# Two gate tiles of the merge projection move from direct products into a thirteenth seven-product pair

## The chip, the cores and the metric

The kernel runs on one core of one Trainium2 chip. The metric is the device time of one execution in microseconds; the number for a kernel is the median of its runs. The profiled execution is a single one, and its page and trace are those of the hardware profiler.

## The reference

One transformer block over 1024 positions of width 1024, in fp32. The part that matters here:

```python
u = rms_norm(h, g_norm_mix[l])
proj = jnp.einsum('btd,de->bte', u, w_in[l]) + b_in[l]
mq, mk, mv, mo, mi, mf, nq, nkv, ngate, merge = split_columns(proj, IN_SIZES)
y_m = mlstm_mixer(mq, mk, mv, mo, mi, mf, b_fgate[l], conv_qk[l], g_mlstm_head[l])
y_n = nsa_mixer(nq, nkv, ngate, pe_cmp[l], w_cmp1[l], w_cmp2[l], rel_bias)
ys = jnp.stack([y_m, y_n], axis=2)
branch = jnp.einsum('btnw,nwd->btnd', ys, w_branch[l])
gates = jax.nn.sigmoid(merge.reshape(B, T, N_BRANCH, D_MODEL))
mixed = jnp.sum(gates * branch, axis=2)
h = h + mixed @ w_out[l]
```

Behind it come a normalised feed-forward layer with three more projections and a last normalisation. `merge`, 2048 columns of the input projection, is the subject: 16 tiles of 128 columns each, needed only when the two branches (mLSTM rows y_m, attention rows y_n) are gated.

## The kernel before

Every fp32 product is made of three passes in a reduced fp32 format: operands are split into a high part (a copy by ACT, ScalarE) and a low part (the rest, by DVE, VectorE), and `mm3` (lines 310 to 313) issues high x high, low x high and high x low. A *direct* tile of 128 columns is 2 halves of 512 positions x 8 slices of depth x 3 matmuls. A *pair* is two such tiles (256 columns) by a Strassen-like scheme: seven products of half the depth (order `QO`: 1, 2, 6, 7, 5, 4, 3), each of 4 slices x 3 matmuls, with sums of weight blocks made beforehand (`sums`, `prep`) and sums of results afterwards (`product`, `finish`), on DVE.

The work runs in stages.

1. **Stage A** (to about 300 us): normalisation, then the twelve pairs in `PAIRS` (line 784), whose two raw weight blocks go to the slots in `RAWS` (line 788) and whose split operands go round a ring of four slots, `WRING`. Beside the pairs run the gates, the compression of keys, and row broadcasts `d_rep` (line 1249, after product 5 of pairs 2 to 9). A planner (`Plan`, line 78) orders all steps by ranks, estimated costs and readiness, engine by engine, when the program is built; each engine then runs its queue in that order, and so does SP's queue, which issues nearly all DMAs. PE is TensorE, POOL is GpSimd.
2. **Heads of the mLSTM** (to about 370 us), same planner. Merge tile 0 is made in stage A; tiles 1 to 3 (`merge_B`, line 1379) are *fill* here: steps of 3 matmuls that the planner puts into PE's holes. Their raw weights go to slot r2, their split parts to the operand ring.
3. **Attention** (to about 680 us): 32 units in an order written out by a second planner (from line 1685): scores, exponentials, scaling, then per group of blocks transposes on PE (tile `T`, two buffers), the high part on ACT (`TH`), the low part on DVE (`TL`), and the products with the values in `obank`. A unit's result goes over `os` to `d_yn` (line 1677). Merge tiles are fill again: `c_dense` (line 1512) yields 16 steps for each of NMC = 10 tiles, `place_dense` (line 1832) puts a step where the planner's clock has PE idle for over 120 ns, and what is left over is issued behind the last unit (line 1902).
4. **Branch stage** (stage D, from line 1950): the remaining two merge tiles, 14 and 15, run first. Into their steps `plan_y` (line 1979) sets the loads and splits of the rows: `load_y(k)` reads the rows y0 to y3 (mLSTM, one part each) and y4 to y7 (attention, two parts each, added by `split_y`) into a ring of six slots; `split_y(k)` makes `YH` on ACT and `YL` on DVE in two halves. `load_gates` reads back the stored merge tiles. Then the products of the branches: `FIRST` (line 2015) is the order for output tiles 0 and 1, all b = 0 products (rows y0 to y3) ahead of the b = 1 products (y4 to y7); `gate` multiplies with the sigmoid on DVE. The tiles 2 to 7 follow one by one.
5. **Output projection, feed-forward, last normalisation** (from line 2080), by the planner again.

The weights of the direct tiles in stages 3 and 4 come through one stream (`Stream`, line 233): a raw load on SP, the high part on ACT, the low part on POOL or DVE.

Of the kernel before, what the change touches and what calls it, by code (L numbers as in the profile page):

```python
# [8 lines left out]
F32 = mybir.dt.float32  # L9
# [5 lines left out]
P = 128  # L15
# [11 lines left out]
C_MQ, C_MK, C_MV, C_MO, C_MI, C_MF = 0, 512, 1024, 1536, 2048, 2052  # L27
C_NQ, C_KV, C_NG, C_MG = 2056, 2568, 3336, 3360
# [6 lines left out]
EPS = 1.0e-6  # L35
MM = 216.0
NTH = 3
NMB, NMX, NMC = 4, 0, 10
FB_ = 400
FB2_ = 1  # L40
NZ_ = 4
# [144 lines left out]
def body(ctx, tc, a, out, stop=None, dbg=None):  # L186
# [113 lines left out]
    def wcols(w, c, n=P):  # L300
        return w.rearrange("(k p) c -> p k c", p=P)[:, :, c:c + n]
# [31 lines left out]
    def wu(ap, scale=None):  # L333
        return ws.add(ap, (KT, P), None, scale)

    j_mg = [wu(wcols(win, C_MG + P * j)) for j in range(16)]
    wbr = a["w_branch"].rearrange("n (k p) c -> p (n k) c", p=P)
    j_br = [wu(wbr[:, :, P * d:P * d + P]) for d in range(8)]

# [23 lines left out]
    with ExitStack() as sa:  # L363
# [417 lines left out]
            load("SP", 256, [(d_mg[t][:, ts_], lambda: o.ap)], [o], [K(True)])  # L781

        QO = (1, 2, 6, 7, 5, 4, 3)
        PAIRS = [("n", 0), ("c", 0), ("q", 0), ("n", 1), ("k", 0), ("s", 0), ("q", 1), ("v", 0), ("k", 1), ("v", 1), ("o", 0), ("o", 1)]
        NP = len(PAIRS)
        COL0 = {"n": C_NQ, "c": C_KC, "q": C_MQ, "k": C_MK, "v": C_MV, "o": C_MO}
        ROW0 = {"n": R_NQ, "q": 0, "k": 4, "v": 8, "o": R_MO}
        RAWS = ["r1 r2", "r0 g20", "g10 r1", "r2 r0", "g20 g10", "r1 r2", "r0 g20", "g10 r1", "r2 r0", "g20 g10", "r1 r2", "r0 g20"]
        WRING = ("w0", "w2", "w1", "w3")
        RB, SB_, OB, keep = {}, {}, {}, {}  # L790
        LO, HI = slice(0, P), slice(P, 2 * P)
# [71 lines left out]
        def store(kb, parts, b, d):  # L863
            load("SP", kb, parts, [b] if isinstance(b, Buf) else b, [d])

        def finish(m, blk, ps, other):
            kind, z = PAIRS[m]
            col, r = blk
            j = 2 * z + col
            bias = COLS[:, R_KV + (col, (2, 4)[col])["cs".index(kind)]:][:, 0:1] if kind in "cs" else COLS[:, ROW0[kind] + j:ROW0[kind] + j + 1]  # L870
            pv, ov = (lambda: ps.ap), (lambda: other.ap)

            def total(cost, view, x):
                o = (lambda: four(other.ap)) if kind in "qk" else ov
                stt(cost, view, (lambda: four(ps.ap)) if kind in "qk" else pv, bias, o, ALU.add, ALU.add, [ps, other, b_c], [x])
            if kind in "qk":
                if (m, col) not in wt:
                    wt[m, col] = slot(order4[turn.setdefault(m, 0)])
                    turn[m] += 1
                w = wt[m, col]  # L880
                total(800.0, lambda: par(flat(w.ap), r), w)
                if (m, col, 1 - r) in wt:
                    conv(m, col)
                wt[m, col, r] = True
                return
            x = out_piece(m)
            v = lambda: x.ap
            if kind == "o":
                ew(V, v, pv, ov, ALU.add, [ps, other], [x])
                stp("ACT", 630.0, lambda: nc.scalar.activation(x.ap, x.ap, AF.Sigmoid, bias=bias), [ps, b_c, tabs[-1]], [x])  # L890
                store(256, [(par(d_mx["o"][j], r), lambda: four(x.ap))], x, dst["o", j])
            else:
                total(760.0, v, x)
                if kind in "cv":
                    d_, db = (d_kc[col], dstc[col]) if kind == "c" else (d_mx["v"][j], dst["v", j])
                    store(256, [(par(d_, r), lambda: four(x.ap))], x, db)
                else:
                    y = out_piece(m, 1)
                    f = -0.125 if kind == "n" else 1.0
                    stp("ACT", 630.0, lambda: nc.scalar.activation(fr(y.ap), x.ap, AF.Copy, scale=f), [x], [y])  # L900
                    if kind == "n":
                        stt(900.0, lambda: fr(x.ap), v, f, lambda: y.ap, ALU.mult, ALU.subtract, [y], [x])
                        ds_, db = [d_q[j][:, zz, :] for zz in range(2)], dstq[j]
                    else:
                        ew(V, lambda: fr(x.ap), v, lambda: y.ap, ALU.subtract, [y], [x])
                        ds_, db = [d_kh[col], d_kl[col]], dsts[col]
                    for d_, t_ in zip(ds_, (y, x)):
                        store(256, [(par(d_, r), lambda t_=t_: four(t_.ap))], t_, db)
            turn[m] += 1
# [325 lines left out]
        for n, (m, q) in enumerate(seq):  # L1235
            kind = PAIRS[m][0]
            if n > 1:
                if q == 1 and n > 13:
                    if m == 2:
                        bias_rows()  # L1240
                        load_raw(2)
                    load_raw(m + 1)
                prep(m, q)
            if (m, q) == (NP - 2, 1):
                table("sigmoid_and_others")
                stp("ACT", 340.0, lambda: nc.scalar.activation(GT[:, :, 0:24], GT[:, :, 0:24], AF.Sigmoid), tabs[-1:], [b_GT])
                stp("DVE", 1360.0, lambda: nc.vector.reciprocal(GT[:, :, 0:24], GT[:, :, 0:24]), (), [b_GT])
            product(m, q)
            if q == 5 and 1 < m < NP - 2:
                load("SP", 983, [(d_rep[m - 2], d_row[m - 2, :].partition_broadcast(P))], [OB[m, q], b_drow], [K(True)], cost=700.0)  # L1250
            if (m, q) == (NP - 1, 4):
                restore()
            if (m, q) == (3, 3):
                compress_0()
                compress(0)
            if (m, q) == (5, 3):
                compress(1)
            if (m, q) == (8, 3):
                head_load(0, "MqkS")
                mask(0)  # L1260
                scale_q(0)
            if (m, q) == (NP - 2, 7):
                head_load(0, "v")
# [656 lines left out]
    def q1_tile(n, dt):  # L1920
        if n not in q1 or q1[n].dtype != dt:
            q1[n] = q1p.tile([P, 4, 512], dt, name=f"q1_{n}_{len(q1)}", tag=f"q1_{n}", bufs=1)
        return q1[n]
# [24 lines left out]
    with ExitStack() as se:  # L1948
# [1 line left out]
        psD = se.enter_context(tc.tile_pool(name="psD", bufs=1, space=PSUM, reuse_waits="tile"))  # L1950
        YH = dp.tile([P, 8, T], F32R, name="YH")
        YL = dp.tile([P, 8, T], F32R, name="YL")
        ring = [q1_tile(n, F32)[:, 2 * z:2 * z + 2, :].rearrange("p a c -> p (a c)") for n in (4, 0, 1) for z in range(2)]
        ys, sgs = {}, {}

        def load_y(*kk):
            for k in kk:
                ys[k] = []
                for src in [d_ym[k]] if k < 4 else [d_yn[0][k - 4], d_yn[1][k - 4]]:
                    ys[k].append(ring.pop(0))  # L1960
                    ring.append(ys[k][-1])
                    nc.sync.dma_start(ys[k][-1], src[:, :])

        def split_y(k):
            y, *more = ys.pop(k)
            for y2 in more:
                nc.vector.tensor_tensor(y, y, y2, ALU.add)
            for half in range(2):
                hs = slice(512 * half, 512 * half + 512)
                split_evict(YH[:, k, hs], YL[:, k, hs], y[:, hs])  # L1970

        def load_gates(d, half):
            hs = slice(512 * half, 512 * half + 512)
            sgs[d, half] = [gring.tile() for b in range(2)]
            for b in range(2):
                nc.sync.dma_start(sgs[d, half][b], d_mg[8 * b + d][:, hs])

        early = Pieces([q1_tile(3, F32)[:, z, :] for z in range(4)])
        plan_y = {(0, 0): [lambda: load_y(0, 1, 2, 3)], (0, 2): [lambda: load_y(4)], (0, 8): [lambda: split_y(0)],
                  (0, 10): [lambda: split_y(1), lambda: load_y(5)], (0, 13): [lambda: split_y(2)], (1, 1): [lambda: split_y(3), lambda: load_y(6)],  # L1980
                  (1, 7): [lambda: split_y(4), lambda: load_y(7)], (1, 12): [lambda: split_y(5)]}
        for n, j in enumerate(range(NMB + NMX + NMC, 16)):
            for z, _ in enumerate(merge_tile(j, gring, psD, 8)):
                for f in plan_y.get((n, z), ()):
                    f()
                if (n, z) == (1, 9):
                    gring, late = early, gring
                    for half in range(2):
                        load_gates(0, half)
                    gring = late  # L1990
# [27 lines left out]
        for d in range(2):  # L2018
            W[d] = ws.get(j_br[d])
        ws.dma(j_br[2])  # L2020
        split_y(6)
        for n, (d, half, b) in enumerate(FIRST):
            x = branch(d, half, b)
            if n == 0:
                split_y(7)
            if n == 6:
                ws.split(j_br[2])
                ws.dma(j_br[3])
            gate(d, half, b, *x)
            if n == 5:  # L2030
                gring.n = 0
                gring, late = early, gring
                load_gates(2, 0)
                gring = late
# [873 lines left out]
```

## Time and profile before

| | |
|---|---|
| median of 3 runs | 1520.71 us (1520.65 to 1521.54) |
| the profiled execution | 1521.38 us |
| its span, first to last instruction | 1519.6 us |
| PE busy | 1507.8 us (99%), 8112 matmuls |
| DVE busy | 1176.0 us (77%) |
| ACT busy | 852.1 us (56%) |
| POOL busy | 174.5 us (11%) |
| moved by DMA | 207.54 MB, 137 GB/s in the mean |

The page gives the busy time of each engine, the span in 40 slices, the DMA queues, the chain of work that ended last (followed back from the last instruction), and groups of instructions. Views of the trace answer closer questions: a table by windows (busy time of each engine between two times), a timeline by engine (start, duration, line, tiles, and in brackets the idle time before and what ended it), and the groups of one tile. Matmuls overlap in the pipe, so a row shows 0.39 us for a matmul while the next starts 0.23 us later. In a row, `d` is the PSUM tile of a direct merge tile in stages 3 and 4, `mg` its evicted result in attention, `br` a branch product, `q` any tile of the ring that the y rows and gates share.

### The profile page before, as it was taken

To read this page: it belongs to the slowest core of one execution; us is meant where nothing else is said; L and a number is where in the kernel's file an instruction comes from. 1 tells how busy PE (TensorE), PEld (TensorE's weight loads), DVE (VectorE), ACT (ScalarE), POOL (GpSimd) and SP (SyncE) were. 2 spreads that over 40 slices of the span, in tenths; PEclk is the share of its full clock that TensorE was granted. 3 is DMA by queue.
4 is the path that set the end of the run, shared out by engine and by line. 5 is a ranking of instruction groups with operands and counts; after the bars stand their busy time and mean duration, and the time that the engine had idled before them with its cause. 6 is when DMAs were issued, how large, how long until landed. Compare 5 with 4: busy or idle time off the path is not lost.

```text
span 1519.6 us, 23351 instructions
## 1 busy us (share of the span) xinstructions
PE 1507.8 (99%) x8112; PEld 1297.1 (85%) x8112; DVE 1176.0 (77%) x2464; ACT 852.1 (56%) x1873; POOL 174.5 (11%) x310
## 2 busy tenths in 40 slices
PE   9999999999999999999999999999999999999997
PEld 8978888888988889888888888888888888888886
DVE  7877889466988798965666598677777778898976
ACT  8535444475988788865444364444444444564443
POOL 7600003333111100011020000000000000110000
PEclk9999999999999999999999999999999999999999
DMA  8458567869232533118456222222222226866002
GB/s 252 156 138 246 190 190 248 227 224 260 76 89 70 156 73 90 41 53 297 139 181 201 84 70 84 76 84 83 84 86 88 84 87 200 282 155 206 1 1 111
DMA packets 164144, 207.54 MB, mean 137 GB/s; under 512 B 10555, under 2 KB 121016, under 8 KB 163771
## 3 DMA queue, kind: packets, MB, share of 16 engines
q1 hardware_dynamic: 152090, 188.22, 38.7%
q0 software_dynamic: 11648, 17.51, 5.9%
q8 instruction: 64, 1.05, 0.3%
q14 instruction: 54, 0.43, 0.1%
q10 hardware_dynamic: 288, 0.33, 0.1%
HBM read 151.34 MB, written 62.48 MB: 141 GB/s over the span
## 4 chain that ended last, share of the span: by engine, by line
PE 96%; DVE 2%; DMA 1%; ACT 1%; issue 1%; DVEq 0%; ACTq 0%; POOLq 0%
PE PS L2323 41%; PE PSA L311 7%; PE PSA L313 6%; PE PSA L312 6%; PE T L1636 4%; PE d L311 3%; PE d L313 3%; PE d L312 3%; PE obank L1667 2%; PE obank L1669 2%; PE PS L313 2%; PE PS L311 2%; PE br L313 2%; PE br L312 2%; PE PS L312 2%; PE br L311 2%
## 5 line engine op out<-in xcount | busy, mean ns | idle before, releaser
L2093 DVE TENSOR_TENSOR sl<-PS,sl 128x512 f32<-128x512 f32 (+1 forms) x186 | 101.2, 559 | 46.2 <-PE PS L2323 32.4
L2323 PE MATMUL PS<-sl,sl 128*128 128x512 f32 (+1 forms) x597 | 129.3, 371 | 0.0
L2323 PEld LDWEIGHTS PS<-sl,sl 128*128 128x128 f32 x597 | 105.8, 188 | 19.5 <-DVE acc L2093 0.2
L1656 DVE TENSOR_TENSOR TL<-T,TH 128x512 fp32r<-128x512 f32 (+1 forms) x151 | 90.6, 617 | 19.3 <-ACT TH L1647 17.6
L2096 ACT ACTIVATE sl<-PS 128x512 f32<-128x512 f32 x72 | 43.0, 598 | 98.5 <-PE PS L2323 96.3
L2096 ACT ACTIVATE sl<-sl 128x512 fp32r<-128x512 f32 (+1 forms) x91 | 56.7, 629 | 70.1 <-DVE sl L2093 48.4
L1647 ACT ACTIVATE TH<-T 128x512 fp32r<-128x512 f32 (+1 forms) x151 | 79.3, 540 | 18.8 <-PE T L1636 17.3
L1667 PE MATMUL obank<-TH,VHL 128*128 128x256 f32 x263 | 75.6, 310 | 0.0
L2093 DVE TENSOR_TENSOR sl<-sl,sl 128x512 fp32r<-128x512 f32 (+1 forms) x90 | 61.6, 686 | 17.4 <-DMA d_h<-sl 8.7
L2323 PE MATMUL PS<-UTH,wl 128*128 128x512 f32 (+1 forms) x272 | 74.8, 346 | 0.0
L311 PE MATMUL d<-UTH,whi 128*128 128x512 f32 x176 | 71.4, 406 | 0.1
L2323 PE MATMUL PS<-q,wh 128*128 128x512 f32 x300 | 70.8, 389 | 0.0
L313 PE MATMUL d<-UTH,wlo 128*128 128x512 f32 x176 | 69.1, 393 | 0.0
L312 PE MATMUL d<-UTL,whi 128*128 128x512 f32 x176 | 69.1, 392 | 0.0
L1669 PE MATMUL obank<-TL,VHL 128*128 128x256 f32 x264 | 68.3, 282 | 0.0
L311 PE MATMUL PSA<-UTH,wOwhi 128*128 128x512 f32 (+1 forms) x172 | 67.1, 390 | 0.0
L313 PE MATMUL PSA<-UTH,wOwlo 128*128 128x512 f32 (+1 forms) x180 | 66.9, 371 | 0.0
L2323 PEld LDWEIGHTS PS<-q,wh 128*128 128x128 f32 x300 | 56.3, 188 | 11.7
L2323 PE MATMUL PS<-UTH,wh 128*128 128x512 f32 (+1 forms) x248 | 66.1, 338 | 0.0
L312 PE MATMUL PSA<-UTL,wOwhi 128*128 128x512 f32 (+1 forms) x172 | 63.7, 370 | 0.0
L2323 PE MATMUL PS<-q,wl 128*128 128x512 f32 x252 | 59.7, 389 | 0.0
L2323 PE MATMUL PS<-q,sl 128*128 128x512 f32 x240 | 57.2, 389 | 0.0
(1389 smaller groups left out, 4561.1 us busy)
## 6 DMA issues: line engine op xcount, KB each, us to landing
d_gu<-sl SPq DMA_DIRECT2D x44, 256.0 KB, 2.3
rA<-in_w_in SPq DMA_DIRECT2D x18, 512.0 KB, 5.6
q<-d_mg SPq DMA_DIRECT2D x32, 256.0 KB, 3.4
d_rep<-d_row SPq DMA_DIRECT2D x8, 960.0 KB, 7.8
ra<-in_w_gate SPq DMA_DIRECT2D x14, 512.0 KB, 5.0
sl<-in_w_up SPq DMA_DIRECT2D x13, 512.0 KB
raw<-in_w_in SPq DMA_DIRECT2D x10, 512.0 KB, 4.9
d_mg<-mg SPq DMA_DIRECT2D x20, 256.0 KB, 2.1
```

The costliest lines, as they stand in the source:

```text
L311: nc.tensor.matmul(ps, ah, bh, start=first, stop=False)
L312: nc.tensor.matmul(ps, ah, bl, start=False, stop=False)
L313: nc.tensor.matmul(ps, al, bh, start=False, stop=last)
L1636: nc.tensor.transpose(pt[:, z, P * r:P * r + P], e, ident)
L1647: nc.scalar.activation(hl[0][:, 0:m], pt[:, 0:m], AF.Copy)
L1656: nc.vector.tensor_tensor(hl[1][:, 0:m], pt[:, 0:m], cast32(hl[0])[:, 0:m], ALU.subtract)
L1667: nc.tensor.matmul(po, vv, th[:, z, :], start=(st[1] == 0), stop=False)
L1669: nc.tensor.matmul(po, vv, tl[:, z, :], start=False, stop=(st[1] == st[2]))
L2093: return pl.step(alts, lambda e: ENG[e].tensor_tensor(out_(), x(), y(), alu), reads, writes, **kw)
L2096: return pl.step((("ACT", cost),), lambda e: nc.scalar.activation(out_(), x(), fn), reads, writes, **kw)
L2323: nc.tensor.matmul(ps, x, y, start=first and n == 0, stop=last and n == 2, skip_group_check=True)
```

## The change

Merge tiles 14 and 15 become pair `("g", 0)` of stage A, between `("k", 1)` and `("v", 1)`: thirteen pairs in place of twelve. Its results get the bias in the sum on DVE and are stored to `d_mg[14]` and `d_mg[15]`. The raw slots of the last pairs shift by one place, so that the last pair uses r1 and r2. Of the tiles 4 to 13, nine (4 to 12) are fill of attention, and one (13) runs at the head of the branch stage. The y rows get a ring of eight slots; y4 and y5 are loaded at once behind y0 to y3, y6 and y7 within the one tile; y0 to y4 are split within it, y5 ahead of the first branch product, y6 behind the first and y7 behind the third. The bank from which the planner of stage 5 starts counting (`n0`, line 2084) follows NMC: 6 in place of 4.

```diff
-NMB, NMX, NMC = 4, 0, 10
+NMB, NMX, NMC = 4, 0, 9
+MG2 = 14
...
-    j_mg = [wu(wcols(win, C_MG + P * j)) for j in range(16)]
+    j_mg = [wu(wcols(win, C_MG + P * j)) for j in range(MG2)]
...
-        PAIRS = [..., ("v", 0), ("k", 1), ("v", 1), ("o", 0), ("o", 1)]
+        PAIRS = [..., ("v", 0), ("k", 1), ("g", 0), ("v", 1), ("o", 0), ("o", 1)]
...
-        RAWS = [..., "g20 g10", "r1 r2", "r0 g20"]
+        RAWS = [..., "g20 g10", "r1 r2", "r0 g20", "r1 r2"]
...
+            bias = COLS[:, R_MG + MG2 + col:R_MG + MG2 + col + 1] if kind == "g" else ...
...
-                if kind in "cv":
+                if kind == "g":
+                    store(256, [(par(d_mg[MG2 + col], r), lambda: four(x.ap))], x, K(True))
+                elif kind in "cv":
...
-            if q == 5 and 1 < m < NP - 2:
+            if q == 5 and 1 < m < 10:
...
-        ring = [... for n in (4, 0, 1) for z in range(2)]
+        ring = [... for n in (4, 0, 1, 2) for z in range(2)]
...
-        plan_y = {(0, 0): [lambda: load_y(0, 1, 2, 3)], (0, 2): [lambda: load_y(4)], (0, 8): [lambda: split_y(0)],
-                  (0, 10): [lambda: split_y(1), lambda: load_y(5)], (0, 13): [lambda: split_y(2)], (1, 1): [lambda: split_y(3), lambda: load_y(6)],
-                  (1, 7): [lambda: split_y(4), lambda: load_y(7)], (1, 12): [lambda: split_y(5)]}
-        for n, j in enumerate(range(NMB + NMX + NMC, 16)):
+        plan_y = {(0, 0): [lambda: load_y(0, 1, 2, 3)], (0, 2): [lambda: load_y(4, 5)], (0, 6): [lambda: split_y(0)],
+                  (0, 8): [lambda: split_y(1), lambda: load_y(6)], (0, 10): [lambda: split_y(2)], (0, 12): [lambda: split_y(3), lambda: load_y(7)],
+                  (0, 14): [lambda: split_y(4)]}
+        for n, j in enumerate(range(NMB + NMX + NMC, MG2)):
...
-                if (n, z) == (1, 9):
+                if (n, z) == (0, 9):
                     gring, late = early, gring
                     for half in range(2):
                         load_gates(0, half)
...
-        split_y(6)
+        split_y(5)
         for n, (d, half, b) in enumerate(FIRST):
             x = branch(d, half, b)
-            if n == 0:
-                split_y(7)
+            if n in (0, 2):
+                split_y((6, 7)[n // 2])
```

More of the change, by code (lines that the diff above doesn't have):

```diff
@@ L783, in body @@
         QO = (1, 2, 6, 7, 5, 4, 3)
-        PAIRS = [("n", 0), ("c", 0), ("q", 0), ("n", 1), ("k", 0), ("s", 0), ("q", 1), ("v", 0), ("k", 1), ("v", 1), ("o", 0), ("o", 1)]
+        PAIRS = [("n", 0), ("c", 0), ("q", 0), ("n", 1), ("k", 0), ("s", 0), ("q", 1), ("v", 0), ("k", 1), ("g", 0), ("v", 1), ("o", 0), ("o", 1)]
         NP = len(PAIRS)
-        COL0 = {"n": C_NQ, "c": C_KC, "q": C_MQ, "k": C_MK, "v": C_MV, "o": C_MO}
+        COL0 = {"n": C_NQ, "c": C_KC, "q": C_MQ, "k": C_MK, "v": C_MV, "o": C_MO, "g": C_MG + P * MG2}
         ROW0 = {"n": R_NQ, "q": 0, "k": 4, "v": 8, "o": R_MO}
-        RAWS = ["r1 r2", "r0 g20", "g10 r1", "r2 r0", "g20 g10", "r1 r2", "r0 g20", "g10 r1", "r2 r0", "g20 g10", "r1 r2", "r0 g20"]
+        RAWS = ["r1 r2", "r0 g20", "g10 r1", "r2 r0", "g20 g10", "r1 r2", "r0 g20", "g10 r1", "r2 r0", "g20 g10", "r1 r2", "r0 g20", "r1 r2"]
         WRING = ("w0", "w2", "w1", "w3")
@@ L869, in finish @@
             j = 2 * z + col
-            bias = COLS[:, R_KV + (col, (2, 4)[col])["cs".index(kind)]:][:, 0:1] if kind in "cs" else COLS[:, ROW0[kind] + j:ROW0[kind] + j + 1]
+            bias = COLS[:, R_MG + MG2 + col:R_MG + MG2 + col + 1] if kind == "g" else COLS[:, R_KV + (col, (2, 4)[col])["cs".index(kind)]:][:, 0:1] if kind in "cs" else COLS[:, ROW0[kind] + j:ROW0[kind] + j + 1]
             pv, ov = (lambda: ps.ap), (lambda: other.ap)
@@ L1952, in body @@
         YL = dp.tile([P, 8, T], F32R, name="YL")
-        ring = [q1_tile(n, F32)[:, 2 * z:2 * z + 2, :].rearrange("p a c -> p (a c)") for n in (4, 0, 1) for z in range(2)]
+        ring = [q1_tile(n, F32)[:, 2 * z:2 * z + 2, :].rearrange("p a c -> p (a c)") for n in (4, 0, 1, 2) for z in range(2)]
         ys, sgs = {}, {}
```

## The prediction

> **What bounds the kernel now.** I read the page's head and chain first.
>
> ```profile
> span 1519.6 us, 23351 instructions
> ...
> PE 96%; DVE 2%; DMA 1%; ACT 1%; issue 1%; DVEq 0%; ACTq 0%; POOLq 0%
> ```
>
> 96% of the chain that ended last is TensorE (PE). So a change pays by the matmuls that it takes from PE, unless it opens a gap there. Next I read the stages that the change touches, in the table by windows: the seven-product pairs (240 to 280) and the end of attention (650 to 675).
>
> ```profile
> 240.00:280.00 40.00, 40.00 (x178) 33.13 (x177) 32.89 (x44) 16.14 (x25) 15.04 (x16) 1.00 0.67 200
> 650.00:675.00 25.00, 25.00 (x169) 22.40 (x168) 20.31 (x57) 18.91 (x51) 1.59 (x4) 1.00 0.21 56
> ```
>
> After the length come busy PE, weight loads, DVE, ACT, POOL, then granted clock, DMA share and GB/s. PE is busy for the whole of both windows and DVE for 82% of the first, 81% of the second: both stages are PE's.
>
> **The matmuls.** The price of one 512-column matmul is read where merge tiles run back to back (first row). The other two rows count the merge matmuls alone in attention's tail and behind it.
>
> ```profile
> 682.09:707.95 25.86, 25.86 (x115) 1.00 0.79 292
> ```
>
> ```profile
> 669.60:680.40 10.80, 6.32 (x24) 4.22 (x24) 0.56 (x1) 1.00 0.33 87
> 680.50:708.20 27.70, 27.54 (x120) 22.44 (x120) 2.81 (x6) 1.00 0.77 285
> ```
>
> 115 starts, the last at the window's end, make 114 steps: 25.86 / 114 = 0.2268 us. A direct merge tile is 2 halves x 8 x 3 = 48 matmuls, two are 96. The pair that replaces them is 7 products x 4 x 3 = 84, in a stage where PE has no hole: 84 x 0.2268 = +19.05 us. By matmuls alone the change wins 12 x 0.2268 = 2.7 us.
>
> Where the 96 go matters more. The tenth fill tile was not all inside attention. Its first half (24 matmuls) was spread over the last 11 us, its second half stood behind attention's last product: 120 matmuls are 2.5 tiles, not 2.
>
> ```profile
> 679.84 0.69 ACT L1449 ACTIVATE mg<-d,COLS 128x512 f32<-128x512 f32 x1 [1.48 <-PE d L313]
> 680.55 0.39 ACT L1675 ACTIVATE os<-obank 128x256 f32<-128x256 f32 x1
> 686.44 0.69 ACT L1449 ACTIVATE mg<-d,COLS 128x512 f32<-128x512 f32 x1 [5.50 <-PE d L313]
> ```
>
> ACT evicts the first half (mg) at 679.84, the last attention output (os) at 680.55, the second half only at 686.44. The planner orders fill only where its clock sees a hole, so with nine tiles the first 144 steps should stay where they are, and the 8 steps of the tail are missing. Behind attention 120 matmuls become 48: 72 x 0.2268 = -16.3 us, sure to leave PE.
>
> **The tail.** The 24 matmuls in it are worth 24 x 0.2268 = 5.4 us, but the chain transposes, ACT high part, DVE low part, product stays. What it can close up is read in DVE's waits there.
>
> ```profile
> 675.04 0.59 DVE L1653 TENSOR_TENSOR TCl<-T,TCh 64x128 fp32r<-64x128 f32 x2 [0.98 <-ACT TCh L1644]
> 676.75 0.69 DVE L1656 TENSOR_TENSOR TL<-T,TH 128x512 fp32r<-128x512 f32 x1 [1.12 <-ACT TH L1647]
> 678.06 1.02 DVE L1656 TENSOR_TENSOR TL<-T,TH 128x512 fp32r<-128x512 f32 x2 [0.62 <-ACT TH L1647]
> ```
>
> These waits, 0.98 + 1.12 + 0.62 = 2.7 us, are for transposes that PE issues behind fill steps. Without fill most of each goes: I take 2.7 us (bounds 0, if the handovers alone set it, and 5.4). The last product then ends, on the old clock without the pair's 19.05, at 680.5 - 2.7 = 677.8. PE path so far: +19.05 - 16.3 - 2.7 = 0.0. The one tile may wait for the bank of os: 0.39 and two handovers, at most 0.7 us.
>
> **The rows of y.** The b = 0 products need y0 to y3, the b = 1 products y4 to y7; all are loaded only after attention and then split by ACT (YH) and DVE (YL).
>
> ```profile
> 680.97 1.24 SPq L1677 DMA_DIRECT2D d_yn<-os  x2
> 687.15 0.33 SPq L1450 DMA_DIRECT2D d_mg<-mg  x1
> 687.57 0.39 SPq L255 DMA_DIRECT2D raw<-in_w_branch  x1
> 688.05 2.33 SPq L1962 DMA_DIRECT2D q<-d_ym  x4
> ```
>
> SP's queue is in order: before, the loads stood behind the store of the left-over half (687.15). Now they stand behind the store of os only: 677.8 + 0.47 + 1.24 + about 0.5 for the weights = 680.0. That is 8 us earlier, while PE wants the rows 16.3 + 2.7 = 19 us earlier. So I follow the rows.
>
> ```profile
> 694.31 3.62 ACT L307 ACTIVATE YH<-q 128x512 fp32r<-128x512 f32 x6 [1.79 <-DMA q<-d_ym]
> ...
> 708.74 1.05 ACT L282 ACTIVATE whi<-raw 128x1024 fp32r<-128x1024 f32 x1
> ```
>
> ```profile
> 694.98 3.76 DVE L308 TENSOR_TENSOR YL<-q,YH 128x512 fp32r<-128x512 f32 x6 [15.90 <-DMA q<-d_ym]
> ...
> 700.62 1.77 DVE L1967 TENSOR_TENSOR q<-q 128x1024 f32<-128x1024 f32 x1 [0.27 <-DMA q<-d_yn]
> ...
> 709.82 1.23 DVE L290 TENSOR_TENSOR wlo<-raw,whi 128x1024 fp32r<-128x1024 f32 x1 [1.16 <-ACT whi L282]
> 710.96 1.22 DVE L1967 TENSOR_TENSOR q<-q 128x1024 f32<-128x1024 f32 x1
> 712.88 1.29 DVE L308 TENSOR_TENSOR YL<-q,YH 128x512 fp32r<-128x512 f32 x2 [0.70 <-ACT YH L307]
> ...
> 716.70 1.29 DVE L308 TENSOR_TENSOR YL<-q,YH 128x512 fp32r<-128x512 f32 x2 [1.39 <-ACT YH L307]
> 717.91 2.48 DVE L2006 TENSOR_TENSOR q<-br,q 128x512 f32<-128x512 f32 x4
> ```
>
> Before: first load issued 688.05, first split 694.31 (6.3 us later), y4's add begins at 700.62 (12.6 later, just after y4 landed), y7's first low half ends at 717.3. Wanted by PE: the branch products begin at 707.95; the fifth is the first with y7, at its fourth k: 707.95 + 4 x 12 x 0.2268 + 10 x 0.2268 = 721.1. Slack 3.8 us.
>
> After, from 680.0: first split 686.3; eight low halves of 3.76 / 6 = 0.63 us from 687.0 end at 692.0, and y4's add starts at 692.2 (the row's 12.6 after issue would be 692.6; y5 now shares the transfer, but a store less does). Then DVE in program order, in its rows' durations: add y4 1.22, wait for ACT's high half 0.7, low halves 1.25: 695.4. ACT has behind y4 the tile's second eviction (0.69) and the high part of the second branch weight (1.05): 694.7 + 1.75 = 696.4. DVE takes that weight's low part (1.23): 697.7. y5: 1.22 + 0.7 + 1.25 = 3.2: 700.9. y6 the same: 704.0. The first two gates, now ahead of y7 in DVE's order, 2 x 2.48 / 4 = 1.24: 705.3. y7's first half: 1.22 + 0.7 + 0.63: 707.9. PE meanwhile: tile from 678.5 to 689.4, two products to 694.8, then the third waits for the weight until 697.7 (2.5 us); it and the fourth end at 702.7, and the fifth, at y7, waits from 705.0 to 707.9 (2.9 us). Without waits it would be there at 702.5. Behind the waiting product all later branch products stand in PE's queue, so nothing fills these gaps; the sigmoids and gates behind the y splits on ACT and DVE come later by as much, without holding PE (eight banks).
>
> The sum: 707.9 - 721.1 + 19.05 = **+5.8 us**. The profiled execution took 1521.38 us (span 1519.6 and 1.8 around it), 0.67 above the median of the runs; applied to the median, 1520.71 + 5.8 = **1526.5 us**. Bounds: no waits at all +0.4; with the whole 5.4 us of the tail too, -2.3; tail not closing up, +8.5.
>
> **Hidden edits.** Raw slot r2 is last used by the new last pair, and the first fill tile of the mLSTM heads loads into it.
>
> ```profile
> 285.83 0.68 DVE L461 TENSOR_TENSOR wOwlo<-Rg,wOwlo 128x512 fp32r<-128x512 f32 x1
> ```
>
> ```profile
> 290.27 2.81 POOL L761 TENSOR_TENSOR wOwlo<-rA,wOwhi 128x256 fp32r<-128x256 f32 x4
> ```
>
> ```profile
> 300.74 0.50 PE L311 MATMUL PSA<-UTH,wOwhi 128*128 128x512 f32 x1
> ```
>
> ```profile
> rA<-in_w_in SPq DMA_DIRECT2D x18, 512.0 KB, 5.6
> ```
>
> The last operand is cut by 286.5; the fill starts at 300.74: 14.2 us for a load (median 5.6), 1.05 on ACT and 2.81 on POOL, 9.5 in all, behind only head loads and stores in SP's queue and the head's masks in POOL's. That leaves 4.7 us of cover; each us beyond it is a us in which PE has only the heads' short matmuls. The pair's splits and sums are DVE's as in any pair, under the 82% of the first window; its four row stores and 1 MB of loads lie in a 0.67 DMA share. The row broadcasts keep their pairs' numbers, and ACT loses four evictions of 0.69 us to DVE's sums: neither is on the path. The shifted bank order of the next stage costs nothing: those banks were emptied products before.
>
> **Clock.** PE at the start, the same eight transposes twice:
>
> ```profile
> 8.67 1.92 PE L596 MATMUL PSA<-cst,XR 128*128 128x128 f32 x8
> ...
> 12.09 1.03 PE L596 MATMUL PSA<-cst,XR 128*128 128x128 f32 x8
> ```
>
> Near 9 us they run at half the pace of 12 us: 1.92 against 1.03. If a wait of 2.5 or 2.9 us brought that back for the 3.4 us between these rows, half of 3.4, 1.7 us, would come on top for each. [...]
>
> **Rivals.**
> - Not slower: the rows come in time. Eight ring slots let y5 load at once, and if the first split starts about 4 us after issue instead of 6.3 and y4's chain runs while DVE waits, the y7 half stands at 702.5. It decides from there. Time 1520.71 + 0.4 = 1521.1. For it: DVE waited 15.90 us at the first load. Against: DVE's own work from the first row to y7's half is 15 x 0.63 + 4 x 1.22 + 1.23 + 1.24 = 16.8 us in one order, and 686.3 + 16.8 is already 703.1. Chance 0.20.
> - The tail does not close up: PE idles where the fill was, everything after starts 2.7 us later: 1529.2. For it: transposes need DVE's low parts two groups back. Chance 0.11.
> - Half clock after the waits: 1.7 more for one, 1528.2. Chance 0.05.
> - The fill of the heads comes late after all, some 3 us with the rest: 1529.5. Chance 0.03.
> - Work that I did not see leaves too: faster than 1517.7. Chance 0.03.
>
> **How the numbers follow.** The forecast, waits of 3 to 7 us in the branch stage, has the remaining 0.58. What a measurement of this kernel can tell from no change is about 0.2%, 3.0 us: 1517.7 to 1523.7. Same: the first rival and the low end of the forecast, 0.23. Faster 0.03: matmuls alone give 2.7. Slower 0.74. Range 1521.0 to 1529.4: from the first rival's time to the second's; what lies outside is half of the first rival, the faster case and the tops of the others, 0.2 together.
>
> **What would show it.** Merge matmuls behind the last attention product: 48. os evicted about 2.7 us sooner, less the shift. First row load about 2.2 us after the last product. PE idle in front of the third branch product (on the weight's low part) and in the fifth (on YL), about 5 us together. Wrong if PE runs through the branch products, if the pair costs more than 19.05, or if PE stands before the heads' first fill.

## The result, and the profile after

| | before | after |
|---|---|---|
| median | 1520.68 us (1519.96 to 1521.54, 4 runs) | 1531.25 us (1530.60 to 1531.70, 4 runs) |
| the profiled execution | 1521.38 us | 1531.66 us |
| its span | 1519.6 us | 1529.9 us |

The ratio is 1.0069 (95% interval 1.0052 to 1.0086): the change makes the kernel 10.6 us slower. The forecast was +5.8.

The head and the chain of the page after:

```profile
span 1529.9 us, 23341 instructions
...
PE 1508.8 (99%) x8100; PEld 1294.6 (85%) x8100; DVE 1188.2 (78%) x2480; ACT 853.1 (56%) x1874; POOL 168.1 (11%) x302
...
PE 90%; DVE 3%; DMA 3%; issue 3%; ACT 1%; SPq 0%; POOL 0%; DVEq 0%; ACTq 0%; POOLq 0%
```

There are twelve matmuls fewer (8100 for 8112), as planned. But PE's share of the chain fell from 96% to 90%: the end now hangs on waits too. To find them I took steps that both kernels have and compared their start times. First PE's timeline of the kernel before, in order: the end of the pairs, a score product of attention's unit 1, one at the head of the tail, one of the tail's last products, a step of the last direct tile, the first matmul with the low part of y7, a step of the feed-forward layer.

```profile
295.90 1.03 PE L1213 MATMUL PSA<-cst,Rg 128*128 128x128 f32 x8
...
377.38 0.47 PE L1542 MATMUL S1s<-KH,QA 128*128 128x512 f32 x1 [0.39 <-DVE nx L1569]
...
661.38 0.48 PE L1542 MATMUL S31s<-KH,QA 128*128 128x512 f32 x1
...
679.64 0.28 PE L1667 MATMUL obank<-TH,VHL 128*128 128x256 f32 x1
...
701.60 0.39 PE L313 MATMUL d<-UTH,wlo 128*128 128x512 f32 x1
...
721.10 0.39 PE L312 MATMUL br<-YL,whi 128*128 128x512 f32 x1
...
1478.46 5.60 PE L2323 MATMUL PS<-sl,sl 128*128 128x512 f32 x24
```

The same steps of the kernel after (its line numbers lie 1 to 3 higher), and among them PE's new waits (those inside the tail come further down):

```profile
314.64 1.04 PE L1216 MATMUL PSA<-cst,Rg 128*128 128x128 f32 x8
...
346.67 0.46 PE L1323 MATMUL PSA<-MSC,XB 128*128 128x129 f32 x2 [0.31 <-DVE MSC L472]
...
354.45 0.63 PE L1377 MATMUL PSA<-cst,XR 128*128 128x128 f32 x4 [0.45 <-DVE XR L1372]
...
356.99 0.66 PE L1377 MATMUL PSA<-cst,XR 128*128 128x128 f32 x4 [0.33 <-ACT RG L781]
...
397.67 0.47 PE L1545 MATMUL S1s<-KH,QA 128*128 128x512 f32 x1 [0.39 <-DVE nx L1572]
...
549.25 0.30 PE L1545 MATMUL S16s<-KH,QA 128*128 128x128 f32 x1 [0.86 <-DVE nx L1572]
...
683.70 0.48 PE L1545 MATMUL S31s<-KH,QA 128*128 128x512 f32 x1
...
699.02 0.28 PE L1670 MATMUL obank<-TH,VHL 128*128 128x256 f32 x1
...
700.50 0.50 PE L312 MATMUL d<-UTH,whi 128*128 128x512 f32 x1 [0.47 <-ACT os L1678]
...
705.18 0.39 PE L314 MATMUL d<-UTH,wlo 128*128 128x512 f32 x1
...
718.90 0.50 PE L312 MATMUL br<-YH,whi 128*128 128x512 f32 x1 [1.69 <-ACT whi L283]
...
720.22 0.50 PE L314 MATMUL br<-YH,wlo 128*128 128x512 f32 x1 [0.58 <-DVE wlo L291]
...
729.47 0.50 PE L312 MATMUL br<-YH,whi 128*128 128x512 f32 x1 [1.93 <-ACT YH L308]
730.20 0.50 PE L313 MATMUL br<-YL,whi 128*128 128x512 f32 x1 [0.22 <-DVE YL L309]
...
833.77 0.66 PE L2256 MATMUL PS<-cst,sl 128*128 128x128 f32 x4 [0.47 <-ACT sl L2249]
...
1488.77 5.60 PE L2326 MATMUL PS<-sl,sl 128*128 128x512 f32 x24
```

The difference of each pair of times, less the one ahead of it, is what the stretch costs:

| stretch | shift at its end | it adds | forecast |
|---|---|---|---|
| start and pairs | +18.74 | +18.74 | +19.05 |
| heads | +20.29 | +1.55 | 0 |
| attention | +22.32 | +2.03 | 0 |
| its tail | +19.38 | -2.94 | -2.7 |
| direct tiles, with the wait for the bank of os | +3.58 | -15.80 | -15.9 |
| branch products up to y7 | +9.10 | +5.52 | +5.4 |
| all behind | +10.31 | +1.21 | 0 |

The forecasts are read off the prediction's own times for PE; they add up to 5.85. Four rows are as forecast within 0.3 us. The excess, 1.55 + 2.03 + 1.21 = 4.8 us, stands in the three rows that I had put at zero.

### The profile page after: what moved, and what is told of

Read it like the earlier page. It is cut to its first block, busy times and chain, and to the rows that moved or that the text cites. A ratio compares the mean times of both kernels' runs of the same rounds, so it can differ in the third digit from the quotient of the medians.

```text
span 1529.9 us, 23341 instructions
## 1 busy us (share of the span) xinstructions
PE 1508.8 (99%) x8100; PEld 1294.6 (85%) x8100; DVE 1188.2 (78%) x2480; ACT 853.1 (56%) x1874; POOL 168.1 (11%) x302
## 4 chain that ended last, share of the span: by engine, by line
PE 90%; DVE 3%; DMA 3%; issue 3%; ACT 1%; SPq 0%; POOL 0%; DVEq 0%; ACTq 0%; POOLq 0%
PE PS L2326 41%; PE PSA L312 7%; PE PSA L314 7%; PE PSA L313 7%; PE T L1639 3%; PE obank L1670 2%; PE obank L1672 2%; PE br L313 2%; PE br L314 2%; PE br L312 2%; PE d L312 2%; PE d L313 2%; PE d L314 2%; PE PS L313 1%; PE PS L312 1%
## 5 line engine op out<-in xcount | busy, mean ns | idle before, releaser
L312 PE MATMUL PSA<-UTH,wOwhi 128*128 128x512 f32 (+1 forms) x188 | 73.2, 389 | 0.0
L313 PE MATMUL PSA<-UTL,wOwhi 128*128 128x512 f32 (+1 forms) x188 | 69.9, 372 | 0.0
L312 PE MATMUL d<-UTH,whi 128*128 128x512 f32 x144 | 58.9, 409 | 0.6 <-ACT os L1678 0.5
L314 PE MATMUL d<-UTH,wlo 128*128 128x512 f32 x144 | 56.6, 393 | 0.0
L313 PE MATMUL d<-UTL,whi 128*128 128x512 f32 x144 | 56.6, 393 | 0.0
```

The costliest lines, as they stand in the source:

```text
L312: nc.tensor.matmul(ps, ah, bh, start=first, stop=False)
L313: nc.tensor.matmul(ps, ah, bl, start=False, stop=False)
L314: nc.tensor.matmul(ps, al, bh, start=False, stop=last)
```

## The experiments

All ratios are to runs of the kernel before on the same chip; a trace shows one execution.

**Another raw slot (e1_slot).**

```diff
-        merge_B(1, ("r2", "w1", "w3"))
+        merge_B(1, ("r0", "w1", "w3"))
```

> The changed kernel, but the first fill tile of the heads (merge tile 1) loads its raw weight into slot r0, which the last pair no longer uses, in place of r2. Theory A (the heads lose their 1.4 us because r2 comes free only behind the last pair, so that the planner issues this load late and orders the heads' loads and fill steps otherwise): the waits of PE between 346 and 357 us (0.31, 0.45, 0.33) go, the first score product of unit 1 starts 18.9 to 19.3 us later than in the kernel before in place of 20.2, and the time falls by 1.1 to 1.4 us, to about 1530.0. Rival B (the thirteenth pair itself shifts the planner's clock, the slot does not matter): waits of about 1 us in the heads stay, 1531 us. If the waits in unit 16 of attention are bad luck of one execution, they are gone here as well.

1531.54 us, ratio 1.0069 (1.0054 to 1.0084). The three waits are gone, but PE now waits 0.75 us at 318.50 and 0.17 at 333.54, and unit 1's score product comes 20.5 us later. So theory A did not show, and B was not proved either: the planner had dealt a third order, as PE's rows show. PE has no wait at unit 16 here. What is new: after the same waits at y7 the matmuls start 0.43 us apart in place of 0.23 (windows, columns as in the prediction):

```profile
728.60:732.40 3.80, 3.54 (x8) 2.63 (x9) 3.73 (x6) 1.57 (x4) 0.00 (x0) 0.55 0.35 106
```

The granted clock is 0.55. By the start times of the same matmuls in the kernel after, the slow stretch cost 1.4 us, about what the gone wait at unit 16 had won.

**The true first bank (e2_n0).**

```diff
-    n0 = (2 * (16 - NMB - NMX - NMC) + 32) % 8
+    n0 = (2 * (MG2 - NMB - NMX - NMC) + 32) % 8
```

> The changed kernel, with the bank from which stage 5 starts counting set to the one that is next by the real count of tiles (2 in place of 6). Theory A (the wrong first bank costs the 0.7 us which the changed kernel loses at the first transposes of stage 5): the wait of 0.47 us on the scaled rows there goes, and the time falls by 0.7 us, to about 1530.5. Rival B (these 0.7 us come from a weight of the output projection and stored rows that landed about 1 us later in one execution): nothing changes, 1531.2 us, and the wait may or may not be there. Up to the end of attention this kernel is the changed one: if PE again stands for about 1 us in unit 16 of attention, that loss is not luck.

1531.0 us, ratio 1.0068 (1.0053 to 1.0083): the same. The wait at 833 is gone here, but it is gone with the wrong bank as well in e1_slot, e5_rows, e6_bias, e9_mid and e11_rev. Where such a wait is there, ACT had stood 1.09 to 1.21 us for a weight of the output projection (after, e4_noadd, e7_last), elsewhere at most 0.73: a late transfer, B. Unit 16's wait, 0.87 us, came again.

**Nine fill tiles without the pair (e3_nine).** The kernel before with

```diff
-NMB, NMX, NMC = 4, 0, 10
+NMB, NMX, NMC = 4, 0, 9
```

> The kernel before with nine fill tiles in attention in place of ten and three tiles behind it; no thirteenth pair, the order of the row loads as before. Theory A (the tail closes up by 2.8 us where its 24 fill matmuls, 5.4 us, are missing, and nothing else changes): 24 more matmuls stand behind attention, +5.4 - 2.8 = +2.7 us, 1523.4 us, the rows come in time, and PE has no wait at unit 16. Rival B (the tail does not close): +5.4, 1526.1. Rival C (the 1.8 us lost around unit 16 come with nine tiles): +4.5, 1525.2, with a wait of about 1 us there.

1524.36 us, ratio 1.0024 (1.0015 to 1.0034), which is 2.3 to 5.2 us. In the trace there is no wait at unit 16, the heads are as before, and the only new wait behind the tail is

```profile
677.39 0.50 PE L311 MATMUL d<-UTH,whi 128*128 128x512 f32 x1 [0.47 <-ACT os L1675]
```

This is A with the 0.47 us of the bank, 3.1 us. In this trace nine tiles alone bring neither the loss in the heads nor the one at unit 16.

**No additions (e4_noadd).** The second part of y4 to y7 is loaded but not added, so it is missing in the result.

```diff
             for y2 in more:
-                nc.vector.tensor_tensor(y, y, y2, ALU.add)
+                pass
```

> The changed kernel without the four additions of the two parts of y4 to y7 on DVE; both parts are still loaded, but the second is left out of the result. Theory A (the order of DVE's work sets when y7 is there): four additions of 1.22 us leave the chain, 4.9 us; PE's wait for the second branch weight shrinks from 2.8 to about 1 us, its wait for y7 goes or stays under 0.5, and the time falls by 4 to 4.5 us, to about 1527. Rival B (the landing of the rows sets it): PE's waits stay at 4 to 5.5 us together and the time at 1530 to 1531.

1530.71 us (1529.32 to 1534.07), ratio 1.0068 (1.0053 to 1.0083). A was right up to y6: there is no wait for the weight, and 0.44 us in two pieces for y6. At y7 it was wrong: something else was late (ACT's timeline):

```profile
722.49 1.28 ACT L2000 ACT_TABLE_LOAD   x1 [4.05 <-DMA q<-d_mg]
...
728.17 0.63 ACT L2000 ACTIVATE q<-q 128x512 f32<-128x512 f32 x1 [2.20 <-DMA q<-d_mg]
728.71 1.13 ACT L308 ACTIVATE YH<-q 128x512 fp32r<-128x512 f32 x2
```

The high part of y7 (YH, the row at 728.71) stands in ACT's order behind a sigmoid, and that waits for a gate tile read back behind the rows. PE then (timeline, and the window behind it):

```profile
729.38 0.80 PE L312 MATMUL br<-YH,whi 128*128 128x512 f32 x1 [2.93 <-ACT YH L308]
```

```profile
729.30:735.40 6.10, 6.02 (x14) 4.42 (x15) 4.48 (x7) 2.73 (x6) 0.00 (x0) 0.50 0.33 99
```

Without four additions the first matmul with y7 begins at 729.38, with them at 729.47; the branch products begin 0.3 us later in this trace, so no more than half a microsecond is won there. The granted clock of 0.50 behind the 2.93 us then cost another 2.5 us. This profiled execution was the slowest of the four, so how often that happens is not shown. In the kernel after the sigmoid lay just ahead of DVE's chain (ACT's timeline):

```profile
727.39 0.63 ACT L2000 ACTIVATE q<-q 128x512 f32<-128x512 f32 x1 [1.26 <-DMA q<-d_mg]
728.79 1.15 ACT L308 ACTIVATE YH<-q 128x512 fp32r<-128x512 f32 x2 [0.76 <-DVE q L1970]
```

ACT is done with the sigmoid there 0.76 us before DVE delivers y7: with the gates landing as they do, a shorter chain on DVE can win no more than that at y7.

**The rows in another order (e5_rows).** `add_y` is the addition, taken out of `split_y`:

```diff
-                  (0, 14): [lambda: split_y(4)]}
...
-                if (n, z) == (0, 9):
+                if (n, z) == (0, 13):
...
-        split_y(5)
+        add_y(4)
+        for k in range(4, 8):
+            if k < 7:
+                add_y(k + 1)
+            split_y(k)
...
-            if n in (0, 2):
-                split_y((6, 7)[n // 2])
```

> The changed kernel with the rows' work in another order: the second branch weight is split ahead of y4; the additions of y4 to y7 stand one row ahead of the splits; all rows are split before the first sigmoid and the first gate; the loads of the first gates stand behind y7 in place of ahead of it. Theory A (PE's waits in the branch products come from the order in which DVE, ACT and the DMA queue do this work): the wait for the second branch weight goes, the wait for y7 falls under 1 us, 4.5 to 5 us in all; a stretch of PE at half clock cannot follow either; time 1526 to 1526.7. Rival B (the rows land too late for any order, 7 MB at about 400 GB/s behind the last attention output): a wait of 2 us or more stays in front of y7, 1528.5 or more.

1529.75 us, ratio 1.0055 (1.0040 to 1.0070). The waits for the second weight are gone, and the rows cost 1.15 us at y6 and 0.24 at y7 in place of 2.15 at y7. A and B both hold in part, for DVE also stood 0.37 and 0.70 us for rows that had not landed. But a later product stood:

```profile
735.51 0.50 PE L312 MATMUL br<-YH,whi 128*128 128x512 f32 x1 [1.06 <-ACT whi L283]
736.77 0.50 PE L314 MATMUL br<-YH,wlo 128*128 128x512 f32 x1 [0.53 <-DVE wlo L291]
```

That is the third weight, whose split stands behind the sigmoids and gates that I had moved back. Seven matmuls at half pace followed, which cost 1.6 us: from 735.5 to 740.7, with the second of these stops in it, the granted clock is 0.68.

**Bias tables (e6_bias).** The edit loads FB of both heads, then FW of both, in place of FB, FW, FB, FW.

```diff
-            for t_, o_, n_ in ((f, 127, T), (w, FX + 127, 640)):
...
+        for what, o_, n_ in ((FB, 127, T), (FW, FX + 127, 640)):
+            for h in (2 * p, 2 * p + 1):
```

> The changed kernel, but for each pair of attention heads both bias tables FB are loaded ahead of both tables FW (before: FB, FW, FB, FW). Theory A (the burst of loads ahead of unit 16 lands 1 to 2 us too late, and DVE stands for the second FB): this FB lands about 0.9 us sooner, PE's wait of 0.86 us at unit 16 falls to nearly nothing, and the time falls by 0.5 to 1.2 us, to about 1530.4. Rival B (unit 16 waits for something else, such as its scores or its keys): the wait stays at 0.4 to 0.9 us, 1531.2.

1530.06 us, ratio 1.0058 (1.0043 to 1.0073). DVE of the kernel after at unit 16:

```profile
546.69 0.29 DVE L1572 CUSTOM_DVE_ANT_0 E16w<-S16w,FB 128x128 f32<-128x128 f32 x1 [2.74 <-DMA FB<-d_rep]
...
548.72 0.29 DVE L1572 CUSTOM_DVE_ANT_0 E16w<-S16w,FB 128x128 f32<-128x128 f32 x1 [1.64 <-DMA FB<-d_rep]
```

and with the new order:

```profile
547.40 0.29 DVE L1573 CUSTOM_DVE_ANT_0 E16w<-S16w,FB 128x128 f32<-128x128 f32 x1 [0.28 <-DMA FB<-d_rep]
```

The second FB is there 1.3 us sooner, and PE's wait for unit 16's scores is gone, here and in all four kernels with this order. With the old order the thirteen-pair kernels have 0.86 (after), none (e1), 0.87 (e2), 0.42 (e4), none (e5), 0.36 (e7), 0.65 (e9), 0.60 (e11). That looks like A, but the traces hold a rival that this run does not rule out. Ahead of the tables SP issues the keys; their last two high parts, before and after:

```profile
513.67 1.14 SPq L1485 DMA_DIRECT2D KH<-d_kh  x2
```

```profile
533.86 2.24 SPq L1488 DMA_DIRECT2D KH<-d_kh  x2
```

In all twelve kernels with thirteen pairs one of these two issues takes 1.10 to 1.73 us, in both with twelve pairs neither takes over 0.59. Where the first of the two is the long one, PE does not wait (e1 and e5 with the old order, and all four with the new one). Where it is the second, PE waits (the other six, all with the old order). So A is not shown: the new order may have met the milder case by luck. The stretch from unit 16's first S16s to unit 19's first S19s shows no gain by the order either: against the kernel before, the four with the new order lose 0.8 to 1.1 us there, e1 and e5 0.5 and 0.7, the other six 1.3 to 1.8. In e6_bias PE also waits 0.54 us for the eviction of a fill tile (mg) just behind. In time alone the gain is not proved (the intervals overlap).

**The pair last (e7_last).**

```diff
-  ... ("k", 1), ("g", 0), ("v", 1), ("o", 0), ("o", 1)]
+  ... ("k", 1), ("v", 1), ("o", 0), ("o", 1), ("g", 0)]
...
-            if (m, q) == (NP - 2, 1):
+            if (m, q) == (NP - 3, 1):
                 table("sigmoid_and_others")
```

> The changed kernel with the new pair at the end of the list of pairs in place of the tenth place, and the table load for the sigmoid one pair earlier. Theory A (the heads' loss of 1.4 us is what the planner's order happens to leave: it was the same with another raw slot, 1.5 us, and another list gives another loss): the first score product of unit 1 comes anywhere between 18.8 and 20.5 us later than in the kernel before, and the time moves with it, 1529.8 to 1531.5. Rival B (the last pairs' results, which the heads need, come too late behind a thirteenth pair in their midst): with the results of the other pairs out 19 us sooner, the waits in the heads go, the shift is 18.8 to 19.1, 1529.8.

1544.74 us, ratio 1.0154 (1.0137 to 1.0171): both theories missed. The planner put another split on POOL ahead of the first loads of attention, which POOL issues (its timeline, then that of the kernel after):

```profile
379.59 3.26 POOL L762 TENSOR_TENSOR wloS<-rA,whiS 128x256 fp32r<-128x256 f32 x4 [24.75 <-ACT whiS L469]
382.80 2.16 POOL L1473 DMA_DIRECT2D QA<-d_q  x4
```

```profile
362.26 2.16 POOL L1473 DMA_DIRECT2D QA<-d_q  x4 [10.21 <-ACT Rg L1314]
```

The loads start 20.5 us later, PE stands 4.67 us for the keys at 397.72, and from 398 to 412 its clock is 0.61.

**Repairs together (e8_both): e5_rows, e6_bias and e2_n0 in one.**

> The changed kernel with the new order of the rows' work, the bias tables in the order FB, FB, FW, FW, and the true first bank in stage 5. If these losses are what they seem, they add up: 4.5 to 5 us from the rows, 0.5 to 1.2 from unit 16, 0 to 0.9 from stage 5: 1524.5 to 1526. By the matmuls alone (19.05 more in the pair, 16.3 fewer behind attention, 2.8 us by which the tail closes up, 0.5 for the bank) it cannot come under 1521. If the rows' landing bounds the branch products, it stays above 1528.

1528.76 us, ratio 1.0050 (1.0035 to 1.0065). It falls short of what I expected by the third weight, 1.10 + 0.52 us again at 736, and by the rows, 1.39 us at y6 and 0.24 at y7.

**The pair in the middle (e9_mid).**

```diff
-  ... ("s", 0), ("q", 1), ("v", 0), ("k", 1), ("g", 0), ("v", 1), ...
+  ... ("s", 0), ("g", 0), ("q", 1), ("v", 0), ("k", 1), ("v", 1), ...
-            if (m, q) == (8, 3):
+            if (m, q) == (9, 3):
                 head_load(0, "MqkS")
```

> The changed kernel with the new pair in the seventh place of the list (behind the keys' pair s) in place of the tenth, and the first head's loads ordered one pair later, so that the pairs of v, k and o and the heads stand to each other as in the kernel before. Theory A (the heads lose 1.4 us because the new pair stands between the pairs on which the first heads wait, and the planner orders heads and fill differently): PE's waits of 0.3 to 0.5 us at 346 to 357 go, the first score product of unit 1 comes 18.9 to 19.3 us later than in the kernel before in place of 20.3, and the time falls by about 1.1 us, to 1530. Rival B (a thirteenth pair shifts the rings of raw weights and operands by one, and this deals the heads' order anew wherever the pair stands): waits of about 1 us stay in the heads, shift 20 to 20.6, 1531.

1530.69 us, ratio 1.0065 (1.0049 to 1.0082). The three waits are there again, 0.31, 0.55 and 0.33 at 346.48, 354.37 and 356.93: A falls. Between the tenth and the seventh place of the list the pair's place does not matter (at its end it does, as e7_last shows). What is left is what its slots do to the end of the list, B.

**The third weight sooner (e10_w2): e8_both and**

```diff
-            if n == 6:
+            if n == 5:
                 ws.split(j_br[2])
```

> The kernel with rows in the new order, bias tables in the new order and the true first bank, and the third branch weight split one product earlier. Theory A (behind the rows the next thing late is this weight, for which PE stood 1.1 and 0.5 us, because its split stands on ACT and DVE behind the sigmoids and gates that came later): these waits go, with about 0.25 us of refilled pipeline for each, 2 us, and the time falls from 1528.8 to about 1526.8. Rival B (the weight cannot be there sooner, since its buffer is the first weight's, which the sixth product still reads): a wait of 1 us or more stays, 1528 or more.

1526.6 us, ratio 1.0039 (1.0024 to 1.0054): A, to 0.2 us. Of the branch stage's waits only 1.08 us at y6 and 0.23 at y7 are left.

**The last pair's blocks exchanged (e11_rev).**

```diff
-  ... "r1 r2", "r0 g20", "r1 r2"]
+  ... "r1 r2", "r0 g20", "r2 r1"]
```

> The changed kernel with the two raw blocks of the last pair exchanged between their slots (r2 r1 in place of r1 r2), so that r2 is free one block sooner; nothing else. In the built program the order of PE's instructions through the heads is then the one of the kernel before, row for row. Theory A (the heads lose 1.3 to 1.4 us because r2 comes free late in the planner's clock, and the order it then deals leaves PE waits of 0.31, 0.45 and 0.33 us at 346 to 357): the waits go, the first score product of unit 1 comes 18.9 to 19.2 us later than in the kernel before in place of 20.3, and the time falls by about 1.2 us, to 1530. Rival B (the order has nothing to do with it; the heads' transfers come later behind thirteen pairs): waits of about 1 us stay somewhere in the heads, shift 20 or more, 1531.

1529.12 us, ratio 1.0052 (1.0038 to 1.0066). No wait in the heads, and unit 1's score product, 397.67 in the kernel after, stands at

```profile
395.71 0.47 PE L1545 MATMUL S1s<-KH,QA 128*128 128x512 f32 x1 [0.39 <-DVE nx L1572]
```

From PE's 0.29 us wait at the head of the heads (299.76, 318.50, 318.21 in before, after and here) to this product it is 77.62, 79.17 and 77.50 us. In the traces PE's matmuls through the heads then stand in the order of the kernel before, one for one; in the kernel after they do not. A is shown as far as this: two exchanged slots give the old order and the 1.55 us back.

**All repairs (e12_best): e10_w2 and e11_rev.**

> All repairs together: the rows in the new order, the third branch weight one product earlier, the bias tables FB, FB, FW, FW, the true first bank, and the last pair's slots exchanged. If the heads' 1.2 us are independent of the rest: 1526.6 - 1.2 = 1525.4. What then remains over the kernel before by the sum of matmuls and waits: the pair +19.05, 72 matmuls behind attention -16.3, the tail -2.8, the bank of the last output +0.5, the wait for y7 about 1.8 with its refills, the wait for an eviction and for a reciprocal around unit 16 about 0.9: +3.1, or 1523.8. Rival (the burst of loads at unit 16 or other transfers take the gain back): 1526 or more. It is not expected to beat the kernel before.

1524.65 us (1523.92 to 1526.49, 11 runs), ratio 1.0023 (1.0014 to 1.0032). That lies between the two sums expected. Of the 10.6 us some 7 are won back; the kernel before stays 2.1 to 4.9 us faster. Nothing that I tried beats it.

## Why the prediction was right and where it failed

**Matmuls: right.** 84 x 0.2268 = 19.05 was forecast for the pair. The first shift, 18.74, holds a start that was 0.30 faster (the same product of a pair stands at 240.36 and 240.06): 19.04. Behind attention stand 48 merge matmuls, in its tail none (windows of the merge tiles alone):

```profile
691.90:700.30 8.40, 0.00 (x0) 0.00 (x0) 0.00 (x0) 1.00 0.16 47
700.40:711.60 11.20, 11.11 (x48) 8.93 (x48) 0.67 (x1) 1.00 0.80 286
```

**The tail: right in size, in part by luck.** It closed up by 2.9 us (2.7), and by as much without the pair, as e3_nine shows. The wait for the bank of os was 0.47 (at most 0.7). But of the three waits of DVE on which the 2.7 rested, 0.98 + 1.12 + 0.62, only the first went wholly (DVE after):

```profile
697.52 1.45 DVE L1659 TENSOR_TENSOR TL<-T,TH 128x512 fp32r<-128x512 f32 x2 [0.68 <-ACT TH L1650]
699.16 0.42 DVE L1659 TENSOR_TENSOR TL<-T,TH 128x256 fp32r<-128x256 f32 x1 [0.19 <-ACT TH L1650]
```

DVE's last low part ended at 679.08 and now ends at 699.58; less the shift of 22.32 at the tail's head that is 1.8 us. The other 1.1 came because PE no longer had fill steps to do between that low part and the last products. PE now waits for DVE in the tail, 1.08 + 0.33 + 0.42 us.

**The rows: right in sum and in kind.** SP's and DVE's timelines:

```profile
702.42 2.21 SPq L1965 DMA_DIRECT2D q<-d_ym  x4
...
709.89 1.83 SPq L1965 DMA_DIRECT2D q<-d_yn  x2
712.31 4.49 SPq L1979 DMA_DIRECT2D q<-d_mg  x4
717.78 0.96 SPq L1965 DMA_DIRECT2D q<-d_yn  x2
```

```profile
714.92 1.23 DVE L1970 TENSOR_TENSOR q<-q 128x1024 f32<-128x1024 f32 x1 [0.65 <-DMA q<-d_yn]
...
718.94 1.23 DVE L291 TENSOR_TENSOR wlo<-raw,whi 128x1024 fp32r<-128x1024 f32 x1 [0.80 <-issue]
...
726.34 1.28 DVE L2009 TENSOR_TENSOR q<-br,q 128x512 f32<-128x512 f32 x2
727.54 1.22 DVE L1970 TENSOR_TENSOR q<-q 128x1024 f32<-128x1024 f32 x1
729.45 1.29 DVE L309 TENSOR_TENSOR YL<-q,YH 128x512 fp32r<-128x512 f32 x2 [0.69 <-ACT YH L308]
```

The first load is issued 2.4 us after the last product (2.2), y4's addition begins 12.5 us behind it (12.2 to 12.6), then weight, gates and y7 follow in the order that was counted out. PE's two stops delayed it by 2.80 and 2.72 us (2.5 and 2.9). In each the longer piece is the wait for the high part on ACT, the shorter one that for the low part, on which the forecast had put it; the low part needs the high one. The brackets show only 1.69 + 0.58 and 1.93 + 0.22: each piece costs some 0.28 us more than its bracket. A bracket counts from the end of the matmul before, 0.39 us after its start and not 0.23, and the second matmul behind a wait starts 0.34 us after the first. What the text missed is how near the next limits were: behind DVE's order stood the sigmoids (e4_noadd), the landing of the rows and the third weight (e5_rows).

**Hidden edits and the terms at zero: here it failed.** The sum has terms for the pair, the tail and the branch stage alone; heads, attention and all behind y7 were put at nothing, and they cost 4.8 us.

For the heads the step was: "Raw slot r2 is last used by the new last pair, and the first fill tile of the mLSTM heads loads into it", "4.7 us of cover". The cover held: the fill began at 319.48, 18.74 us later like all else. But I had asked whether the tile comes in time, not what the planner does with a slot that its clock sees free later. It ordered the heads' loads, fill steps and short matmuls anew, in an order with 1.55 us of waits and refills (e9_mid, e11_rev). That the slots did it is shown; that r2 coming free late on the planner's clock is the reason is argued, not shown.

For attention the step was that "the first 144 steps should stay where they are". The largest zero stood here, 2.03 us, and 1.8 of it around unit 16: DVE's second use of FB there comes at 548.72, against 526.67 in the kernel before and a shift of 20.20 until then. SP's issue of the keys ahead of it took 1.1 us longer than there (0.7 to 1.2 in every kernel with thirteen pairs, nothing in the other one with twelve), and the second FB was issued 2.1 us later. Why the issue takes longer, and where the last 0.2 us of attention come from, stays open.

Behind y7 0.5 us are spread over the branch stage and the output projection, and 0.7 came from a transfer that was late in this execution, in two others and not in the rest (e2_n0). "The shifted bank order ... costs nothing" was right (e2_n0).

**Clock.** The sum has no term for half pace, and the rival with one such stretch had a chance of 0.05: both were my estimate, and no run shows a stop length up to which the clock stays full. In the profiled execution it did stay so (granted clock 1.00 in the window from 729.4 to 737). With the same order of the branch stage it did not in two others: 0.55 from 728.6 to 732.4 in e1_slot, behind y7, and 0.50 from 719.4 to 722.5 in e6_bias, behind the second weight (last section). In e1_slot it cost 1.4 us; my 1.7 for one was near. In e6_bias it cost nothing in sum, for y7 was not there sooner anyway: PE's wait for its high part shrank from 1.93 us to 0.49.

## What to carry to other kernels

Work that is moved out of a filler's place must leave behind what it had hidden: here 16 us of matmuls left the spot that covered the rows' loads, and a third of them came back as waits. Where a planner deals the order from readiness, an edit to a slot can cost more than its own cover: build both orders and compare them before any step is put at zero. A chain that is shortened on one engine should be priced up to the next engine's order, not to zero. And before a wait that goes is credited to an edit, look in the traces for what else differs ahead of it, as at unit 16.

## What the runs showed of the hardware

Behind stops of 2 to 3 us PE's granted clock was about half in some executions and full in others. In e6_bias PE stood 1.48 and 0.58 us, with two matmuls between, and then the clock was 0.50:

```profile
719.40:722.50 3.10, 3.04 (x7) 2.49 (x8) 2.40 (x5) 1.91 (x3) 0.00 (x0) 0.50 1.06 414
```

In the kernel after, PE stood 1.69 and 0.58 us at the same place, with two matmuls between, and the clock was 1.00:

```profile
718.90:723.00 4.10, 3.51 (x14) 2.62 (x15) 3.36 (x4) 1.65 (x3) 0.00 (x0) 1.00 1.05 409
```

At y7 it was 0.55 in e1_slot and 1.00 in the kernel after, behind the same waits, and 0.50 in e4_noadd behind 2.93 us. At the third weight PE stood 1.06 + 0.53 us in e5_rows and 1.10 + 0.52 in e8_both; the mean granted clock of the profiled execution is 0.997 in the first, 0.999 in the second. What decides between half and full pace is not shown.
